# A two-layer hybrid decoder: gates from seven half-size products, seeded accumulators, values and merged sum in DRAM, stages in another order

## The chip, the cores and the metric

The kernel runs on one core of a Trainium2 chip. Its five engines work side by side, each through its own queue: TensorE (PE, with PEld for its weight loads), VectorE (DVE), ScalarE (ACT), GpSimd (POOL) and SyncE (SP, which here only issues transfers). The metric is the time of one execution on the device in microseconds (us). Three executions before took 1969.81, 1969.9 and 1974.25 us, a median of 1969.9.

## The reference

There are 512 tokens with 1024 channels, in float32, and two layers. Cut to what matters:

```python
mod = c_act @ w_ada[l] + b_ada[l]                # 6 x 1024 modulation values
h = rms_norm(x, norm1[l]) * (1.0 + sc1) + sh1
q, k, v, g, u, vs, p, gate_cols = split_columns(h @ w_in[l])
y_ret  = retention(q, k, v, g, positions)        # 4 heads, rotary, decay, rms norm, silu(g)
y_sgu  = spatial_gating(u, vs, ...)              # gelu(u) * (W_s rms_norm(gelu(vs)) + b)
y_pool = multiscale_pool(p, w_pool[l], ...)      # windows 2, 4, 8, 16
branch_proj = einsum('bsnc,ncd->bsnd', stack([y_ret, y_sgu, y_pool]), w_branch[l])
merged = sum(sigmoid(gate_cols) * branch_proj, over the three branches)
x = x + gt1 * (merged @ w_out[l])
h2 = rms_norm(x, norm2[l]) * (1.0 + sc2) + sh2
x = x + gt2 * (square(relu(h2 @ w_ff1[l])) @ w_ff2[l])    # 4096 hidden channels
```

After both layers comes a last rms norm. The gates are 3 x 1024 columns of `w_in`.

## The kernel before

Activations lie channels by tokens: 8 blocks of 128 partitions with 512 tokens. Every large product is made from three, in `mm3` (L405): each float32 operand is split into a high part (ScalarE, `act`, L210) and a low part, the rest (VectorE, `ttn`, L207), and high x high, high x low and low x high are added up in PSUM. So `a_unit`, 128 output channels from 1024 input channels, is 8 x 3 = 24 matmuls of 512 columns.

The weights come in **units** of 128 x 1024 (512 KB), in the order in which they are used. SP loads them (L226) into four buffers. A unit is split as two halves of 512, with eight such half buffers.

`pair` is another way to make two such output blocks at once. It takes them as a 2 x 2 block product (two halves of the tokens, two of the input channels) and makes it from seven half-size products rather than eight: sums S1 to S4 of weight blocks by sums T1 to T4 of activation blocks. Each product is 4 blocks x 3 = 12 matmuls of 256 columns into one of four PSUM banks a, b, c and d; VectorE adds the banks up. The T sums are made once per activation (`Halved.add`), the S sums per pair: S1 and S3 on POOL, S2 and S4 on VectorE (L274). Before, only the first feed-forward product uses pairs, 11 in each layer; the gates are direct units.

The stages of a layer before: v; vs; retention by heads (q, k, g, scores, with `attend` and `attend_norm` of one head during the next); branch 0 (each gate, then its branch product, which VectorE multiplies into `merged`); u with the spatial gating; branch 1; p; the pooling product `wpool`; branch 2; the output product; then the feed-forward part in four quarters of the hidden channels, `ff1` and `ff2` in turn. Between them lie 96 **modulation units**: a unit of `w_ada` is loaded and reduced on VectorE (L245), one after each step that carries `mods=1`.

Order: `run()` goes through the steps, and before each step it has the weights of the next LOOKAHEAD halves loaded and split. A scheduler then places the instructions of each engine, each engine works strictly in that order, and waits only for what an instruction reads or overwrites. At the passages between layers and sub-layers the order is written out by hand (`ordered` steps).

Of the kernel before, what the change touches and what calls it, by code (L numbers as in the profile page):

```python
# [11 lines left out]
F32 = mybir.dt.float32  # L12
# [5 lines left out]
P = 128  # L18
D = 1024
# [96 lines left out]
class Weights:  # L116


    def __init__(self, halves):
        self.halves = halves  # L120

    def part(self, i, o, n):
        return self.halves[o // S][i][:, o % S:o % S + n]
# [8 lines left out]
class Halved:  # L132
# [6 lines left out]
    def add(self, p, f):  # L139

        b = self.b
        upper, lower = f
        r11, r12, r21, r22 = upper[:, :, :HT], upper[:, :, HT:], lower[:, :, :HT], lower[:, :, HT:]
        for names in (("T1", "T2"), ("T3", "T4")):
            raw = b.b4("tsum").rearrange("p a (k s) -> p a k s", k=2)
            x, y = raw[:, 0], raw[:, 1]
            if names[0] == "T1":
                b.ttn(x, r11, r12, ALU.subtract)
                b.ttn(y, r22, x, ALU.add)
                t2 = y  # L150
            else:
                b.ttn(x, r12, r22, ALU.subtract)
                b.ttn(y, r21, t2, ALU.subtract)
            parts = [b.big.tile([P, 2, 2, HT], F32R, tag="b4", name=b.name("tpart")) for _ in range(2)]
            b.act(parts[0], raw, AF.Copy)
            b.ttn(parts[1], raw, parts[0].bitcast(F32), ALU.subtract)
            for i, n in enumerate(names):
                self.sums[n, p] = [t[:, i] for t in parts]
# [9 lines left out]
class Builder:  # L168
    def __init__(self, tc, ctx, ins, out, wstream, order):
# [8 lines left out]
        self.whl = ctx.enter_context(tc.tile_pool(name="whl", bufs=HALF_BUFS))  # L178
# [15 lines left out]
    def tt(self, s="t", dt=F32):  # L194
        return self.tmp.tile([P, S], dt, tag="t", name=self.name(s))

    def bank(self):
        return self.psum.tile([P, S], F32, tag="ps", name=self.name("ps"))

# [29 lines left out]
    def half(self):  # L229
        return tuple(self.whl.tile([P, S], F32R, tag="w" + w, name=self.name("w" + w)) for w in ("hi", "lo"))  # L230

    def split_half(self, src):
        hi, lo = self.half()
        self.act(hi, src, AF.Copy)
        self.ttn(lo, src, hi.bitcast(F32), ALU.subtract)
        return hi, lo

    def load_unit(self, key, early=False):
# [10 lines left out]
        def parts(between=None):  # L249
            src = [raw[:, i * S:(i + 1) * S] for i in range(2)]  # L250
            if between is None:
                return Weights([self.split_half(x) for x in src])
            halves = [self.half() for _ in src]
            for x, (hi, _) in zip(src, halves):
                self.act(hi, x, AF.Copy)

            def low():
                for x, (hi, lo) in zip(src, halves):
                    self.ttn(lo, x, hi.bitcast(F32), ALU.subtract)

            between()
            return Weights(halves), low
# [3 lines left out]
    def load_pair(self, keys):  # L266
# [3 lines left out]
        sums = {}  # L270

        def add(name, x, y, eng):
            sums[name] = self.sums.tile([P, S], F32, tag="sum", name=self.name("sum"))
            eng.tensor_tensor(sums[name], x, y, ALU.add)  # L274
            return sums[name]

        def make(form):
            nc = self.nc
# [987 lines left out]
```

## Time and profile before

The profiled execution took 1971.48 us by the same clock as the runs, with a span of 1969.8 us. The granted TensorE clock is 0.995 of full speed on the mean.

| engine | busy us | share of the span |
|---|---|---|
| PE | 1943.2 | 99% |
| DVE | 1224.8 | 62% |
| ACT | 789.0 | 40% |
| POOL | 85.4 | 4% |

The transfers move 237.95 MB, a mean of 121 GB/s. Busy times of matmuls overlap, so a busy PE is not PE at its peak; what a matmul costs is read from the distance between starts in the timeline. In a row of waits stand engine, tile and line, what it waited for, then total us, number of times and the longest. In a row of groups stand total us and mean ns of one, then the idle time before them and what ended it.

### The profile page before, as it was taken

To read this page: it belongs to the slowest core of one execution; us is meant where nothing else is said; L and a number is where in the kernel's file an instruction comes from. 1 tells how busy PE (TensorE), PEld (TensorE's weight loads), DVE (VectorE), ACT (ScalarE), POOL (GpSimd) and SP (SyncE) were. 2 spreads that over 40 slices of the span, in tenths; PEclk is the share of its full clock that TensorE was granted. 3 is DMA by queue.
4 is the path that set the end of the run, shared out by engine and by line. 5 is a ranking of instruction groups with operands and counts; after the bars stand their busy time and mean duration, and the time that the engine had idled before them with its cause. 6 is when DMAs were issued, how large, how long until landed. Compare 5 with 4: busy or idle time off the path is not lost.

```text
span 1969.8 us, 25044 instructions
## 1 busy us (share of the span) xinstructions
PE 1943.2 (99%) x9632; PEld 1635.6 (83%) x9632; DVE 1224.8 (62%) x2089; ACT 789.0 (40%) x1290; POOL 85.4 (4%) x90
## 2 busy tenths in 40 slices
PE   8999999999999989999999999999999999999998
PEld 5887788788888879898888777888888898899896
DVE  7757755646744697797652675344375458666665
ACT  4434332323433454353534334233243336353442
POOL 2000000000000001111000000000000000102010
PEclk9999999999999999999999999999999999999999
DMA  8322454444323254654423232222232212332331
GB/s 349 127 87 78 148 179 169 151 155 147 97 97 97 72 178 150 201 181 153 137 87 129 86 100 78 101 86 97 97 96 97 96 65 97 107 118 74 120 107 43
DMA packets 67818, 237.95 MB, mean 121 GB/s; under 512 B 7537, under 2 KB 9713, under 8 KB 67698
## 3 DMA queue, kind: packets, MB, share of 16 engines
q1 hardware_dynamic: 67698, 236.35, 35.9%
q8 instruction: 75, 1.23, 0.3%
q14 instruction: 45, 0.37, 0.1%
HBM read 234.23 MB, written 2.10 MB: 120 GB/s over the span
## 4 chain that ended last, share of the span: by engine, by line
PE 93%; DVE 3%; DMA 2%; ACT 1%; issue 1%; SPq 0%; POOL 0%; DVEq 0%; ACTq 0%
PE ps L405 89%; DMA raw<-in_weights 2%; PE ps L792 2%; PE ps L769 1%; PE ps L885 1%; DVE wlo L207 1%; ACT whi L210 0%; PE ps L987 0%; PE ps L805 0%; DVE raw L245 0%; DVE s L207 0%; DVE tsum L207 0%; ACT tpart L210 0%; DVE fo L204 0%; SPq L488 0%
## 5 line engine op out<-in xcount | busy, mean ns | idle before, releaser
L210 ACT ACTIVATE whi<-raw 128x512 fp32r<-128x512 f32 x658 | 406.8, 629 | 798.0 <-PE ps L405 671.8
L207 DVE TENSOR_TENSOR wlo<-raw,whi 128x512 fp32r<-128x512 f32 x658 | 454.9, 700 | 328.1 <-ACT whi L210 324.3
L405 PE MATMUL ps<-h_hi,whi 128*128 128x512 f32 x896 | 356.5, 398 | 0.0
L405 PE MATMUL ps<-h_hi,wlo 128*128 128x512 f32 x896 | 349.9, 391 | 0.0
L405 PE MATMUL ps<-h_lo,whi 128*128 128x512 f32 x896 | 349.6, 390 | 0.0
L405 PE MATMUL ps<-hid_lo,whi 128*128 128x512 f32 (+1 forms) x544 | 204.8, 377 | 0.0
L405 PE MATMUL ps<-hid_hi,wlo 128*128 128x512 f32 (+1 forms) x544 | 204.6, 377 | 0.0
L405 PE MATMUL ps<-hid_hi,whi 128*128 128x512 f32 (+1 forms) x544 | 203.6, 378 | 0.5 <-ACT whi L210 0.5
L405 PEld LDWEIGHTS ps<-h_hi,whi 128*128 128x128 f32 x896 | 168.9, 189 | 36.5 <-issue 2.4
L405 PEld LDWEIGHTS ps<-h_lo,whi 128*128 128x128 f32 x896 | 168.9, 189 | 36.4 <-issue 2.6
L405 PEld LDWEIGHTS ps<-h_hi,wlo 128*128 128x128 f32 x896 | 168.6, 188 | 35.4
L245 DVE CUSTOM_DVE_ANT_0 raw<-raw,cact 128x1024 f32<-128x1024 f32 x96 | 117.3, 1223 | 115.6 <-DMA raw<-in_weights 115.6
L405 PE MATMUL ps<-hh_hi,whi 128*128 128x256 f32 (+1 forms) x456 | 141.0, 315 | 3.1 <-ACT whi L210 3.1
L405 PE MATMUL ps<-hh_lo,whi 128*128 128x256 f32 (+1 forms) x456 | 142.5, 313 | 0.0
L405 PE MATMUL ps<-hh_hi,wlo 128*128 128x256 f32 (+1 forms) x456 | 141.8, 313 | 0.0
L405 PE MATMUL ps<-tpart,whi 128*128 128x256 f32 x704 | 129.3, 285 | 0.0
L405 PEld LDWEIGHTS ps<-hid_hi,whi 128*128 128x128 f32 x544 | 102.4, 188 | 19.1 <-ACT whi L210 0.7
L405 PEld LDWEIGHTS ps<-hid_hi,wlo 128*128 128x128 f32 x544 | 102.4, 188 | 18.6
L405 PEld LDWEIGHTS ps<-hid_lo,whi 128*128 128x128 f32 x544 | 102.4, 188 | 18.4
L405 PEld LDWEIGHTS ps<-tpart,whi 128*128 128x128 f32 x704 | 111.2, 194 | 0.5
L204 DVE SCALAR_TENSOR_TENSOR x<-ps,mod,x 128x512 f32<-128x512 f32 (+1 forms) x88 | 61.3, 700 | 67.4 <-PE ps L405 67.3
L405 PE MATMUL ps<-tpart,wlo 128*128 128x256 f32 x352 | 99.9, 286 | 2.6 <-DVE wlo L207 2.6
(186 smaller groups left out, 3104.8 us busy)
## 6 DMA issues: line engine op xcount, KB each, us to landing
raw<-in_weights SPq DMA_DIRECT2D x436, 512.0 KB, 3.5
x<-in_xT SPq DMA_DIRECT2D x8, 256.0 KB, 4.0
dec<-in_decay SPq DMA_DIRECT2D x4, 512.0 KB, 6.4
out_dram<-fo SPq DMA_DIRECT2D x8, 256.0 KB, 2.1
mix<-in_wsT SPq DMA_DIRECT2D x2, 256.0 KB, 6.9
mix<-in_bs SPq DMA_DIRECT2D x2, 256.0 KB, 6.9
posi<-in_positions SPq DMA_DIRECT2D x1, 256.0 KB, 10.3
vecs<-in_vecs SPq DMA_DIRECT2D x1, 92.0 KB, 1.9
```

The source lines that it names most:

```text
L204: self.nc.vector.scalar_tensor_tensor(out, in0, sc, in1, op0, op1)
L207: self.nc.vector.tensor_tensor(out, a, b, op)
L210: self.nc.scalar.activation(out, in_, f, **k)
L245: self.nc.vector.tensor_tensor_reduce(out=raw, in0=raw, in1=self.cact, scale=0.5, scalar=0.0, op0=ALU.mult, op1=ALU.add, accum_out=acc)
L405: mm(ps, lhsT=l, rhs=r, start=start and i == 0, stop=stop and i == 2, skip_group_check=loose)
L769: nc.tensor.matmul(ps[:, :w], lhsT=k[:, j * P:(j + 1) * P], rhs=q[:, j * P:], start=True, stop=True)
L792: nc.tensor.matmul(ps[:, j * P:], lhsT=st["v"][j][:, col // S, col % S:col % S + P], rhs=sc[j], start=j == 0, stop=j == NCH - 1)
L885: nc.tensor.matmul(mx[:, t * P:(t + 1) * P], lhsT=st["vg"][t][:, c // 4, (c % 4) * P:(c % 4) * P + P], rhs=st["wsr"][t // 2][:, t % 2, g * ...
```

## The change

All three branches' gates are made as pairs (12 in each layer), over T sums of `h` that are made during the vs steps. In the feed-forward part four output blocks of the second quarter become direct units, where two were, so 10 pairs are left there.

Inside `pair` ScalarE seeds accumulators: after the first product bank a is copied to b, product S2 then adds onto b, b is copied to c, and S3, S4 and W2b go onto b, c and b again. Product S1 goes to d and is copied to SBUF, from where VectorE adds it to two outputs. Two PSUM banks form a pool of their own for seeded banks (b and c), and six stay in the old one.

Units are split whole (1024 columns, four buffers), the weight sums are all on VectorE, two of them in place over the loaded unit, and POOL adds nothing. LOOKAHEAD becomes two whole units.

The values v are stored to DRAM after their stage and loaded again by heads; the decay table is loaded for two heads at a time; `merged` is stored to DRAM after branches 1 and 0 and loaded again. The stages become: v, vs, u, branch 1, retention, branch 0, p, `wpool`, branch 2. The square of the direct feed-forward units moves from VectorE to ScalarE, and feed-forward pairs carry no modulation units; branch 1 carries them in both layers and branch 0 in the first only.

```diff
@@ class Weights, constants
-LOOKAHEAD = 4
-HALF_BUFS = 8
-BIG_BUFS = 30
+LOOKAHEAD = 2
+UNIT_BUFS = 4
+BIG_BUFS = 31
-PAIR_AHEAD = 7
-FORMS = ("W1a", "S2", "S1", "S3", "W1b", "S4", "W2b")
+FORMS = {"W1a": (0, 0), "W1b": (0, S), "S1": (1, 0), "S2": (1, S), "S3": (2, 0), "S4": (2, S), "W2b": (3, 0)}
...
@@ class Halved: the sums of the activations
-    def add(self, p, f):
+    def add(self, p, f=None):
+        if f is None:
+            f = []
+            for k2 in (p, p + KB // 4):
+                f.append(b.b4("f32"))
+                hi, lo = (self.act.two(w, k2).bitcast(F32) for w in ("hi", "lo"))
+                b.ttn(f[-1], hi, lo, ALU.add)
...
+        b.ttn(t1, r12, r11, ALU.subtract)
+        b.ttn(t2, r22, t1, ALU.subtract)
+        b.ttn(t3, r22, r12, ALU.subtract)
+        b.ttn(t4, r21, t2, ALU.subtract)
...
@@ pools
-        self.sums = ctx.enter_context(tc.tile_pool(name="sums", bufs=3))
-        self.pairs = ctx.enter_context(tc.tile_pool(name="pairs", bufs=1))
+        self.sums = ctx.enter_context(tc.tile_pool(name="sums", bufs=1))
+        self.dram = ctx.enter_context(tc.tile_pool(name="dram", bufs=1, space=bass.MemoryType.DRAM))
-        self.psum = ctx.enter_context(tc.tile_pool(name="psum", bufs=8, space=bass.MemoryType.PSUM))
+        self.psum = ctx.enter_context(tc.tile_pool(name="psum", bufs=6, space=bass.MemoryType.PSUM))
+        self.seeded = ctx.enter_context(tc.tile_pool(name="seeded", bufs=2, space=bass.MemoryType.PSUM))
...
@@ splitting a unit, and the weight sums of a pair
-    def split_half(self, src):
-        hi, lo = self.half()
-        self.act(hi, src, AF.Copy)
-        self.ttn(lo, src, hi.bitcast(F32), ALU.subtract)
+    def split_unit(self, src):
+        n = src.shape[-1]
+        hi, lo = self.unit()
+        self.act(hi[:, :n], src, AF.Copy)
+        self.ttn(lo[:, :n], src, hi[:, :n].bitcast(F32), ALU.subtract)
+        return Weights(hi, lo)
...
-            if form == "W1a":
-                add("S1", r2[:, a], r2[:, b], nc.gpsimd)
-                add("S3", r1[:, a], r2[:, a], nc.gpsimd)
-                src = r1[:, a]
...
+            if group == 0:
+                return self.split_unit(r1)
+            if group == 1:
+                s = self.sums.tile([P, D], F32, tag="sum", name=self.name("sum"))
+                got.append(s)
+                self.ttn(s[:, a], r2[:, a], r2[:, b], ALU.add)
+                self.ttn(s[:, b], s[:, a], r1[:, a], ALU.subtract)
+                return self.split_unit(s)
+            if group == 2:
+                self.ttn(r1[:, a], r1[:, a], r2[:, a], ALU.subtract)
+                self.ttn(r1[:, b], r1[:, b], got[0][:, b], ALU.subtract)
+                return self.split_unit(r1)
+            return self.split_unit(r2[:, b])
...
@@ pair
-        a, b, c, d = (self.bank()[:, :HT] for _ in range(4))
+        a, b, c, d = (x()[:, :HT] for x in (self.bank, self.ubank, self.ubank, self.bank))
...
         product(a, "W1a", "R11", True)
-        self.act(a1, a, AF.Copy)
-        product(b, "S2", "T2", True)
-        self.ttn(q, b, a1, ALU.subtract)
-        product(c, "S1", "T1", True)
-        self.ttn(r, q, c, ALU.subtract)
-        product(d, "S3", "T3", True)
-        self.ttn(out1[:, h1], r, d, ALU.add)
+        self.act(b, a, AF.Copy)
+        product(d, "S1", "T1", True)
+        self.act(d_sb, d, AF.Copy)
+        product(b, "S2", "T2", False)
+        self.act(c, b, AF.Copy)
         product(a, "W1b", "R21", False)
-        self.act(out0[:, h0], a, f)
+        f(out[:, 0, h0], a)
+        product(b, "S3", "T3", False)
+        self.ttn(out[:, 1, h1], b, d_sb, ALU.add)
         product(c, "S4", "R22", False)
-        self.ttn(out0[:, h1], c, q, ALU.subtract)
-        product(d, "W2b", "T4", False)
-        self.ttn(out1[:, h0], d, q, ALU.add)
+        self.ttn(out[:, 0, h1], c, d_sb, ALU.add)
+        product(b, "W2b", "T4", False)
+        f(out[:, 1, h0], b)
...
@@ mixer: v, T sums of h, retention, gates, branches
-            st["v"] = []
+            st["v"] = self.dram.tile([NCH, P, D], F32, tag="v", name=self.name("v"))
...
-                st["v"].append(vt)
+                nc.sync.dma_start(out=st["v"][t], in_=vt.rearrange("p a s -> p (a s)"))
...
+                if n == 1 and k2 in (0, 2):
+                    hx.add(k2 // 2)
...
+                if what == "q":
+                    if hd % 2 == 0:
+                        self.dec = self.b4("dec")
+                        nc.sync.dma_start(out=self.dec, in_=self.ins["decay"][:, hd:hd + 2, :])
+                    vh = self.b4("vh").rearrange("p a (b e) -> p (a b) e", b=2)
+                    nc.sync.dma_start(out=vh, in_=st["v"][:, :, hd * 256:(hd + 1) * 256].rearrange("t p e -> p t e"))
...
-                ps = self.a_unit(w, h)
-                t = self.tt("gate")
-                self.act(t, ps, AF.Tanh, scale=0.5)
-                st["gate", c] = t
+                g = self.b4("gate")
...
+                self.pair(form, hx, g, tanh, hooks)
+                tanh(g[:, :, HT:], g[:, :, HT:])
...
+                if n != 1 and i == 0 and k2 + 1 < KB // 2:
+                    recall(0 if n == 2 else 1, k2 + 1)
                 ps = self.a_unit(w, y)
...
+                elif i == 1:
+                    nc.sync.dma_start(out=parked[n, k2], in_=merged[k2].rearrange("p a s -> p (a s)"))
...
         def branch(n, y, mods=0):
-            ahead = 3 if n == 0 else 1
+            ahead = 2 if n == 0 else 1
+            for k2 in range(ahead):
+                gates(n, k2, mods)
+            for k2 in range(KB // 2):
+                for c in (2 * k2, 2 * k2 + 1):
+                    self.step([("A", "w_branch", l, n, 0, c * P)], branch_step(n, y, c), mods=mods)
+                if k2 + ahead < KB // 2:
+                    gates(n, k2 + ahead, mods)
-        branch(0, yret, mods=1)
...
-        branch(1, ysgu, mods=1 if l == 0 else 0)
+        branch(1, ysgu, mods=1)
+        retention()
+        branch(0, yret, mods=1 if l == 0 else 0)
...
+        for k2 in range(KB // 2):
+            for j in ((0,), (1, 2, 3), (), ())[k2]:
+                gates(2, j)
+            if k2 == 0:
+                self.step([("P", "w_pool", l, 1, 0, 0)], wpool_step(4))
+            for c in (2 * k2, 2 * k2 + 1):
+                self.step([("A", "w_branch", l, 2, 0, c * P)], branch_step(2, ypool, c))
...
@@ channel mixer
-            self.ttn(s, r, r, ALU.mult)
+            self.act(s, r, AF.Square)
...
-                if (q, k2) == (1, 0):
-                    for c in range(2):
-                        self.step([wff1(q, c)], ff1_step(q, c), mods=1)
+                if q == 1 and k2 < 2:
+                    for c in (2 * k2, 2 * k2 + 1):
+                        self.step([wff1(q, c)], ff1_step(q, c))
                 else:
-                    self.step([("pair", wff1(q, 2 * k2), wff1(q, 2 * k2 + 1))], ff1_pair(q, k2), mods=1)
+                    self.step([("pair", wff1(q, 2 * k2), wff1(q, 2 * k2 + 1))], ff1_pair(q, k2))
```

Three places of the order.

VectorE, end of the u steps and begin of the second branch in layer 0 (`ysg` and `ysgu0_lo3` are the last block of that branch's input, `wlo` low parts of weights, `raw ... cact` with `acc` and `mod` a modulation unit). Before:

```order
L245 ISA raw_594_3010,acc0_96<-raw_594_3010,cact_100 128x1024
L245 ISA acc0_96 128x1
L207 TENSOR_TENSOR wlo_576_2921<-raw_574_2918,whi_575_2920 128x512
L313 TENSOR_TENSOR mod0_98<-acc0_96,vecs_83 128x1
L207 TENSOR_TENSOR wlo_578_2925<-raw_574_2918,whi_577_2924 128x512
L204 SCALAR_TENSOR_TENSOR ysg_565_2872<-ps_564_2867,vecs_83,mix_128_662 128x512
L207 TENSOR_TENSOR ysg_565_2872<-ysg_565_2872,gu_563_2865 128x512
L207 TENSOR_TENSOR ysgu0_lo3_2824<-ysg_565_2872,ysgu0_hi3_2822 128x512
```

After:

```order
L256 ISA raw_236_1416,acc0_98<-raw_236_1416,cact_102 128x1024
L256 ISA acc0_98 128x1
L217 TENSOR_TENSOR wlo_227_1352<-raw_204_1224,whi_226_1351 128x512
L304 TENSOR_SCALAR mod0_100<-acc0_98,vecs_85 128x1
L214 SCALAR_TENSOR_TENSOR ysg_217_1308<-ps_216_1303,vecs_85,mix_107_623 128x512
L305 TENSOR_TENSOR mod0_100<-mod0_100,vecs_85 128x1
L217 TENSOR_TENSOR ysg_217_1308<-ysg_217_1308,gu_215_1301 128x512
L217 TENSOR_TENSOR ysgu0_lo3_1267<-ysg_217_1308,ysgu0_hi3_1265 128x512
L217 TENSOR_TENSOR sum_243_1483<-raw_238_1436 128x512
L217 TENSOR_TENSOR sum_243_1483<-sum_243_1483,raw_237_1434 128x512
```

Before, a modulation unit and two half splits stand ahead of the last block; now a modulation unit and one half split do, and behind it come the weight sums (`sum`) of a gate pair.

SP, second branch in layer 0 after the change (`raw` are weight units, `parked` the place of `merged` in DRAM):

```order
L236 DMA raw_290_1800<-in_weights 128x1024
L236 DMA raw_291_1818<-in_weights 128x1024
L236 DMA raw_294_1824<-in_weights 128x1024
L886 DMA parked_7_113<-merged_270_1660 128x1024
L236 DMA raw_295_1841<-in_weights 128x1024
L236 DMA raw_296_1843<-in_weights 128x1024
L236 DMA raw_315_1966<-in_weights 128x1024
```

The store of the second part of `merged` now stands between unit loads. It waits for VectorE's last product into `merged_270_1660`, and the load behind it (`raw_295_1841`) for the buffer of `raw_267_1640`, which VectorE's next instruction sets free:

```order
L217 TENSOR_TENSOR wlo_274_1691<-sum_272_1687,whi_273_1690 128x1024
L305 TENSOR_TENSOR mod0_100<-mod0_100,vecs_85 128x1
L217 TENSOR_TENSOR wlo_283_1743<-raw_266_1638,whi_282_1742 128x1024
L214 SCALAR_TENSOR_TENSOR merged_270_1660<-gate_247_1517,ps_275_1694 128x512
L217 TENSOR_TENSOR wlo_285_1760<-raw_267_1640,whi_284_1759 128x512
L256 ISA raw_294_1824,acc0_98<-raw_294_1824,cact_102 128x1024
```

The fourth row is that product and the fifth the instruction that frees the buffer.

ScalarE in a run of feed-forward pairs of layer 0 (`whi` high parts of weights, `pair` the outputs, `hid0_2_hi2` their high part, `a1` the copy of bank a; after the change `us` are the seeded banks and `d` the copy of bank d). Before:

```order
L210 ACTIVATE whi_1379_7271<-sum_1371_7216 128x512
L210 ACTIVATE pair_1330_7033<-pair_1330_7033 128x1024
L210 ACTIVATE whi_1381_7288<-raw_1368_7210 128x512
L210 ACTIVATE hid0_2_hi2_7178<-pair_1330_7033 128x1024
L210 ACTIVATE whi_1384_7307<-sum_1383_7305 128x512
L210 ACTIVATE whi_1393_7337<-raw_1369_7212 128x512
L210 ACTIVATE whi_1397_7360<-raw_1396_7358 128x512
L210 ACTIVATE pair_1358_7182<-ps_1359_7183 128x256
L210 ACTIVATE a1_1391_7335<-ps_1387_7331 128x256
L210 ACTIVATE whi_1399_7364<-raw_1396_7358 128x512
```

After:

```order
L220 ACTIVATE us_994_6248<-ps_993_6247 128x256
L220 ACTIVATE d_997_6251<-ps_996_6250 128x256
L220 ACTIVATE whi_1004_6318<-raw_1002_6314 128x1024
L220 ACTIVATE us_995_6249<-us_994_6248 128x256
L220 ACTIVATE whi_1007_6338<-sum_1006_6335 128x1024
L220 ACTIVATE pair_992_6246<-ps_993_6247 128x256
L220 ACTIVATE whi_1009_6357<-raw_1002_6314 128x1024
L220 ACTIVATE pair_992_6246<-pair_992_6246 128x2x256
L220 ACTIVATE us_1013_6382<-ps_1012_6381 128x256
L220 ACTIVATE d_1016_6385<-ps_1015_6384 128x256
```

Before, one copy of bank a stands among half splits, and VectorE takes the other sums from the banks. Now three copies are made per pair, the one of bank b to c (`us_995_6249<-us_994_6248`) behind the whole split `whi_1004_6318` of the next pair.

More of the change, by code (lines that the diff above doesn't have):

```diff
@@ L249, in parts @@
         def parts(between=None):
-            src = [raw[:, i * S:(i + 1) * S] for i in range(2)]
             if between is None:
[L252 to L259, printed above, removed]
+                return self.split_unit(raw)
+            hi, lo = self.unit()
+            self.act(hi, raw, AF.Copy)
             between()
-            return Weights(halves), low
+            return Weights(hi, lo), lambda: self.ttn(lo, raw, hi.bitcast(F32), ALU.subtract)
         return mod if key[0] == "mod" else parts
@@ L330, in run @@
             for k in keys:
[L331 removed]
+                pieces += [(k, g) for g in range(4)] if k[0] == "pair" else [(k, None)]
             pieces += [(mod_queue.pop(0), None) for _ in range(min(mods, len(mod_queue)))]
```

232 lines of the change are left out of this document (106 added, 126 removed).

## The prediction

> **What bounds the kernel now.** I read the page's totals first, then the chain of waits, then TensorE's waits, then single stages.
>
> ```profile
> span 1969.8 us, 25044 instructions
> PE 1943.2 (99%) x9632; PEld 1635.6 (83%) x9632; DVE 1224.8 (62%) x2089; ACT 789.0 (40%) x1290; POOL 85.4 (4%) x90
> ...
> PE 93%; DVE 3%; DMA 2%; ACT 1%; issue 1%; SPq 0%; POOL 0%; DVEq 0%; ACTq 0%
> ```
>
> TensorE is busy all the time and is 93% of the chain. So the time falls only by fewer or cheaper matmuls, or by the waits that TensorE still has:
>
> ```profile
> PE ps L405 <- ACT whi L210: 3.6, 8, 1.0
> PE ps L405 <- ACT ysgu_hi L210: 3.5, 1, 3.5
> PE ps L405 <- DVE wlo L207: 2.6, 1, 2.6
> PE ps L474 <- DMA cin<-in_c: 2.3, 1, 2.3
> PE ps L805 <- DVE osq L204: 1.7, 1, 1.7
> ```
>
> The other five rows of that view add 4.2, so all waits are 17.9 us of the span. The rest is matmuls back to back, and what one costs is its spacing in the timeline, not its "busy" mean (matmuls overlap):
>
> ```profile
> 602.77 0.39 PE L405 MATMUL ps<-mrg_lo,whi 128*128 128x512 f32 x1
> ...
> 608.89 0.39 PE L405 MATMUL ps<-mrg_lo,whi 128*128 128x512 f32 x1
> 839.15 0.28 PE L405 MATMUL ps<-hh_hi,whi 128*128 128x256 f32 x1
> ...
> 844.90 0.28 PE L405 MATMUL ps<-hh_hi,whi 128*128 128x256 f32 x1
> ```
>
> The first two rows are 27 steps apart: 6.12/27 = 0.2267 us for 512 columns. The second two are 48 steps apart (four products of twelve): 5.75/48 = 0.120 us for 256 columns.
>
> How near the other engines are to TensorE is read by stage. The columns are length, then busy time of PE, PEld, DVE, ACT and POOL, then the granted clock, the DMA share and GB/s:
>
> ```profile
> 134.00:251.00 117.00, 115.28 (x485) 88.88 (x484) 82.51 (x146) 46.16 (x68) 0.00 (x0) 1.00 0.33 109
> 373.00:461.00 88.00, 84.53 (x360) 68.92 (x359) 47.54 (x92) 25.10 (x44) 0.11 (x1) 0.96 0.51 168
> 690.00:722.00 32.00, 26.87 (x145) 22.73 (x144) 31.56 (x54) 20.15 (x38) 3.45 (x2) 0.95 0.33 109
> 839.00:877.00 38.00, 38.00 (x316) 37.92 (x315) 35.56 (x62) 23.41 (x40) 6.75 (x4) 1.00 0.49 161
> ```
>
> The rows are the v and vs steps, the second branch, the passage into the first FF pair, and a run of FF pairs, all of layer 0. VectorE is full only in the third (31.56 of 32), and there TensorE falls behind. At 35.56 of 38 TensorE is still full.
>
> **Matmuls.** A pair is 7 products of 12 matmuls of 256 columns, 84 x 0.120 = 10.08 us, in place of two direct units, 48 x 0.2267 = 10.88. It gains 0.80. The instruction order has 6860 matmuls of 512 columns before and 5804 after, 2464 of 256 before and 4312 after, the rest alike: 1056 go, 1848 come, which is 22 pairs (24 gate pairs in, 2 FF pairs out). 1056 x 0.2267 - 1848 x 0.120 = 239.4 - 221.8, so **-17.6**. All of it lies on the bounding engine.
>
> The Trainium skill ("TensorE: Matmul & The Clock Gate", "Back-to-back issue gap") gives columns/2.4 + 2.5 ns as the gap of isolated matmuls. By it 215.8 and 109.2 ns, 227.9 - 201.8 = 26.1 us saved and a result near 1949; the rows are 5% and 10% longer here, so the measurement decides.
>
> **Stalls that go.** Two of the waits stand where the change rearranges work. The second branch:
>
> ```profile
> 376.39 1.23 DVE L245 CUSTOM_DVE_ANT_0 raw<-raw,cact 128x1024 f32<-128x1024 f32 x1 [2.03 <-DMA raw<-in_weights]
> 377.54 0.08 DVE L245 DVE_READ_ACCUMULATOR2_ANT acc<- 128x1 f32 x1
> ...
> 378.14 0.15 DVE L313 TENSOR_TENSOR mod<-acc,vecs 128x1 f32<-128x1 f32 x1
> ...
> 381.07 0.79 PE L405 MATMUL ps<-ysgu_hi,whi 128*128 128x512 f32 x1 [3.47 <-ACT ysgu_hi L210]
> ```
>
> VectorE sat 2.03 us on a modulation unit's load, then made two weight splits, and only then the last block of `ysgu`; one direct gate (24 x 0.2267 = 5.4 us) did not cover that. The stage's clock of 0.96 is another 0.04 x 88 = 3.5. After the change a gate pair of 10.1 us stands there, 4.6 us more cover than a 3.5 us wait needs: **-7.0**. The other is the first FF pair:
>
> ```profile
> 710.23 0.38 PE L405 MATMUL ps<-tpart,wlo 128*128 128x256 f32 x1 [2.55 <-DVE wlo L207]
> ...
> 712.01 0.63 PE L405 MATMUL ps<-tpart,whi 128*128 128x256 f32 x2
> 712.43 0.41 PE L405 MATMUL ps<-tpart,wlo 128*128 128x256 f32 x1
> ```
>
> Two matmuls take 0.42 there, 0.21 each, nearly twice 0.120: the clock is halved behind a 2.55 us wait (0.95 over the 32 us is 1.6 more). The change puts four direct units ahead of that pair and takes eight squares and the modulation units off VectorE: **-4.2**.
>
> The Trainium skill ("TensorE: Matmul & The Clock Gate", "Part 1: The HAM clock gate") puts the fall to half clock behind an idle window of about 3.4 us; here 2.55 us sufficed, so I price every wait of 2.5 us and more with a half clock behind it. By the page alone waits under 3.4 us would cost only themselves, and the third rival below would come to about 1961 (12.0 of waits in place of 8.0).
>
> **What VectorE and ScalarE get.** Durations by group:
>
> ```profile
> L207 DVE TENSOR_TENSOR hid_lo<-pair,hid_hi 128x1024 fp32r<-128x1024 f32 x22 | 26.9, 1223 | 4.5 <-ACT hid_hi L210 4.2
> L207 DVE TENSOR_TENSOR wlo<-raw,whi 128x512 fp32r<-128x512 f32 x658 | 454.9, 700 | 328.1 <-ACT whi L210 324.3 <-PE ps L405 0.8
> L207 DVE TENSOR_TENSOR merged<-merged,gate 128x512 f32<-128x512 f32 x32 | 22.0, 686 | 0.0
> L207 DVE TENSOR_TENSOR pair<-ps,qr 128x256 f32<-128x256 f32 x44 | 18.3, 418 | 20.1 <-PE ps L405 20.1
> L274 DVE TENSOR_TENSOR sum<-sum,raw 128x512 f32<-128x512 f32 x44 | 37.7, 856 | 9.9 <-POOL sum L274 9.4
> L245 DVE CUSTOM_DVE_ANT_0 raw<-raw,cact 128x1024 f32<-128x1024 f32 x96 | 117.3, 1223 | 115.6 <-DMA raw<-in_weights 115.6
> L210 ACT ACTIVATE hid_hi<-pair 128x1024 fp32r<-128x1024 f32 x22 | 23.1, 1050 | 0.2
> L210 ACT ACTIVATE whi<-raw 128x512 fp32r<-128x512 f32 x658 | 406.8, 629 | 798.0 <-PE ps L405 671.8 <-issue 73.2 <-DMA raw<-in_weights 41.7
> L210 ACT ACTIVATE a<-ps 128x256 f32<-128x256 f32 x22 | 8.1, 368 | 0.0
> L210 ACT ACTIVATE r<-ps 128x512 f32<-128x512 f32 x20 | 11.3, 597 | 4.8 <-PE ps L405 3.4 <-DVE hid_lo L207 1.2
> L210 ACT ACTIVATE sq<-x 128x512 f32<-128x512 f32 (+1 forms) x48 | 25.9, 557 | 38.6 <-DVE x L204 37.7 <-DVE ntot L207 0.9
> raw<-in_weights SPq DMA_DIRECT2D x436, 512.0 KB, 3.5
> dec<-in_decay SPq DMA_DIRECT2D x4, 512.0 KB, 6.4
> ```
>
> VectorE in one FF pair after: three whole-unit low parts 3 x 1.223, one half 0.700, four weight sums 4 x 0.686, two outputs 2 x 0.418, the hidden low part 1.223: 9.17 of TensorE's 10.08, 91%, under the 94% of the run of pairs that was full. (The old weight sums took 0.856 beside POOL's; at that price it would be 9.85, still under 10.08.) ScalarE has 3 x 1.050 + 0.629 for splits, five copies and outputs of 256 columns at 0.368, one relu at about 0.597, square and high part at 1.050 each: 8.3 of 10.08. A gate pair with its two products and three modulation units: 7.95 + 3 x (1.223 + 0.08 + 0.15) + 2 x (1.223 + 0.686) = 16.1 of 10.08 + 2 x 5.44 = 20.96. One load's wait as long as the row of a unit's load (3.5) fits into the 4.9 us left. So I charge VectorE nothing in the steady stages. The T sums of `h` (8 additions at 0.686, 4 low parts and 4 additions of 1024 columns at 1.223, 15 us a layer) go into the v and vs steps, where 117 - 82.5 = 34 us are free: nothing; without that cover, up to 30 us.
>
> The 48 more transfers (v stored and loaded by heads, `merged` parked) are 24 MB on queues that are busy a third of the time. Each parking store waits on SP for a VectorE product, with weight loads queued behind it; but in the order the load next behind waits for the very next VectorE instruction, so the store holds up nothing. A load of v or decay (6.4 us at worst) is issued with its head's q step, and `scores`, the first to need it, comes three units, 16 us, later. Nothing again; if a load did come late, some 3.5 us each.
>
> **New waits,** none of them in the trace, so bounded by rows:
> - At the end of FF quarter 0, ScalarE now does relu, square, high part (0.597 + 0.557 + 0.629) for eight blocks among splits of 1.05, and the next units wait for banks and high parts: 0 to 6 a layer; I take 3, for two layers 6.0, less the 3.6 of `whi` waits that stand mostly there: **+2.4**.
> - Within a run of FF pairs (3, 4 and 3 a layer) the seed `c` is copied from `b` after product S2, and S3 overwrites `b` 12 x 0.120 = 1.44 us later. In the order one split stands ahead of the copy: 1.05 + 0.37 + 0.1 = 1.52, so 0.08 late, filled by two matmuls of the next pair; a second split would make it 1.13. I take 0.35, nearer the low end, on the 14 pairs that have a predecessor: **+4.9**. (The other seed, of `b` from `a`, has only itself, 0.37, to do in the 1.44 of product S1: nothing.)
> - Branch 0 now follows retention with all gate pairs around the last head's `attend`; the nearest row is the 1.7 of `osq`: 0 to 4.5 (with half clock) a layer, taken 1.5: **+3.0**.
> - From `p` through `wpool` into three gate pairs in a row (VectorE makes pools, splits and sums there); the nearest row is the 2.6 of the first FF pair: 0 to 4.5, taken 2.5 a layer: **+5.0**.
> - The first unit is split whole: 1.050 - 0.629 + 1.223 - 0.700: **+0.9**.
>
> Sum on the profiled execution, whose own time is 1971.5: 1971.5 - 17.6 - 7.0 - 4.2 + 2.4 + 4.9 + 3.0 + 5.0 + 0.9 = 1958.9. That execution lies 1.6 over the median of 1969.9, so **1957**.
>
> **Rivals.**
> 1. No new wait at all: 1971.5 - 28.8 - 1.6 = 1941, or 1943 with half a microsecond lost here and there. For it: every new wait sits beside slack of several microseconds in the steady stages. Against: a queue in program order keeps a late item in front. 0.18.
> 2. Slower: the accumulator hand-off. If two splits stand in front of the copy of `b` in every pair, 2 x 1.05 + 0.37 - 1.44 = 1.03 us a pair, 44 pairs: 1957 - 4.9 + 45.3 = 1997. It decides from (1969.9 - 1952.4)/44 = 0.40 us a pair. For it: the copy exists nowhere in the old pair, where four banks let each product be read at leisure. Against: only one split stands there in the order. 0.14, reaching down to 1976.
> 3. No change: the gain is given back at transitions. Waits of 3 us with half a clock of 1.6 behind at the four places of the third and fourth point, 18.4 in place of 8.0: 1957 + 10.4 = 1968. For it: both stalls of before were of this kind. Against: pairs give twice the cover of a direct gate. 0.20.
>
> That the change would not remove the matmuls is excluded by the counts.
>
> **How the numbers follow.** The forecast, 1946 to 1966, has 0.48. A measurement of this kernel tells 0.3%, 5.9 us, from no change: bounds 1964.0 and 1975.8. Faster: rival 1 and nine tenths of the forecast, 0.18 + 0.43, and a tenth of rival 3, 0.02: 0.63. Same: 0.05 of the forecast, 0.16 of rival 3: 0.21. Slower: rival 2, 0.14, and a tenth of rival 3, 0.02: 0.16. The range, 1942 to 1976, takes in rivals 1 and 3, leaves out the slower one and a little below. The ends of all bounds together are 1941 and, with 0.5 for each of 44 pairs, 6 and 18 for the transitions, about 1988.
>
> **What would show it.** TensorE's matmul spacing stays 0.227 and 0.120; the waits on `ysgu_hi` and on the first FF pair's `wlo` are gone; waits on the seeded banks appear in FF runs with some 0.3 us each; the granted clock is 1.00 in the second branch. VectorE stays under 95% in FF runs. Wrong it would be if TensorE waited half a microsecond or more in each pair, if waits on DMA or on parked tiles appeared, or if spacing within a pair grew.

## The result and the profile after

The changed kernel took 1986.8 us (median of four runs, 1984.92 to 1987.02) against 1971.3 (1969.81 to 1974.25): a ratio of 1.0075, with a 95% interval of 1.0057 to 1.0092. The forecast was 1957 with a range of 1942 to 1976. It is slower, and not by the mechanism of any of the three rivals.

The page of the changed kernel, totals and chain:

```profile
span 1984.9 us, 25937 instructions
...
PE 1930.0 (97%) x10424; PEld 1660.5 (84%) x10424; DVE 1293.1 (65%) x1895; ACT 817.4 (41%) x1156; POOL 19.7 (1%) x46
...
PE 89%; DVE 5%; DMA 3%; ACT 2%; issue 1%; SPq 0%; POOL 0%; DVEq 0%; ACTq 0%
```

TensorE is 89% of the chain, where it was 93%, and VectorE and the transfers stand there with 5% and 3%. TensorE's waits say for what:

```profile
PE ps L912 <- DVE wsr L1182: 28.3, 2, 16.0
PE ps L406 <- ACT r L220: 7.0, 2, 3.5
PE ps L477 <- DMA cin<-in_c: 2.4, 1, 2.4
PE us L406 <- DVE pair L217: 1.3, 2, 1.1
...
PE us L406 <- ACT us L220: 0.9, 2, 0.5
...
PE ps L406 <- DVE wlo L217: 0.7, 3, 0.3
PE ps L406 <- ACT whi L220: 0.7, 2, 0.6
```

All waits add up to 45.2 us (three rows of 1.3, 1.1 and 0.9 and three of 0.2 are not shown), against 17.9 before. The span grew by 15.1. With the 17.6 that the matmul counts save, 32.7 have to be found: 27.3 are more waits. The remaining 5.4 were not placed: the granted clock is lower, 0.990 on the mean against 0.995, but that mean also counts time in which TensorE only waited.

The first row is new. `wsr` are the weights of the spatial gating, scaled by the statistics of vs, one wait in each layer. The stretch of the first one in the windows (columns as in the prediction):

```profile
96.00:132.00 36.00, 19.96 (x88) 16.29 (x87) 32.21 (x54) 12.40 (x15) 0.00 (x0) 0.80 0.54 167
```

TensorE is busy for 20 of 36 us, VectorE for 32. TensorE's timeline there:

```profile
114.45 0.39 PE L406 MATMUL ps<-h_hi,wlo 128*128 128x512 f32 x1
130.87 0.79 PE L912 MATMUL ps<-wsr,vg 128*128 128x128 f32 x2 [16.04 <-DVE wsr L1182]
131.32 0.77 PE L406 MATMUL ps<-h_hi,whi 128*128 128x512 f32 x1
131.89 0.63 PE L406 MATMUL ps<-h_lo,whi 128*128 128x512 f32 x1
```

and VectorE's, with ScalarE's last gelu of vs ahead of it:

```profile
111.96 0.58 ACT L220 ACTIVATE vg<-ps 128x512 f32<-128x512 f32 x1
```

```profile
112.62 1.23 DVE L256 CUSTOM_DVE_ANT_0 raw<-raw,cact 128x1024 f32<-128x1024 f32 x1 [1.66 <-DMA raw<-in_weights]
...
117.39 1.23 DVE L256 CUSTOM_DVE_ANT_0 raw<-raw,cact 128x1024 f32<-128x1024 f32 x1 [0.54 <-DMA raw<-in_weights]
...
118.54 1.22 DVE L217 TENSOR_TENSOR tpart<-tsum,tpart 128x1024 fp32r<-128x1024 f32 x1
119.67 1.22 DVE L1173 CUSTOM_DVE_ANT_0 junk<-vg 128x1024 f32<-128x1024 f32 x1
...
125.64 1.22 DVE L1173 CUSTOM_DVE_ANT_0 junk<-vg 128x1024 f32<-128x1024 f32 x1
...
128.48 1.23 DVE L256 CUSTOM_DVE_ANT_0 raw<-raw,cact 128x1024 f32<-128x1024 f32 x1 [1.41 <-DMA raw<-in_weights]
...
130.33 1.67 DVE L1182 TENSOR_SCALAR wsr<-mix,vss 128x512 f32<-128x512 f32 x4
```

The last block of vs is there at 112.5. Then VectorE has modulation units, T sums and weight splits in its queue, makes the four sums of squares (`junk`) from 119.67 to 126.8, and `wsr` from 130.33. TensorE came to the first mixing matmul at 114.8, since u now follows vs directly, and everything behind it waited.

Before, the same matmul came 200 us later, and the row was in the trace of before:

```profile
116.19 1.68 DVE L1153 TENSOR_SCALAR wsr<-mix,vss 128x512 f32<-128x512 f32 x4
```

```profile
321.91 1.05 PE L885 MATMUL ps<-wsr,vg 128*128 128x128 f32 x8
```

`wsr` was ready at 117.9 and first used at 321.9, with retention and branch 0 between. That cover is what the new order of the stages took away.

The move alone does not give the size of the wait. In the trace of before vs ends here, and the next unit begins:

```profile
110.42 0.39 PE L405 MATMUL ps<-whi,h_lo 128*128 128x512 f32 x1
110.65 0.39 PE L405 MATMUL ps<-h_hi,whi 128*128 128x512 f32 x1
```

From there to the first `wsr` at 116.19 are 5.5 us, and one unit is 5.4. With VectorE's queue as it was, u directly behind vs would have waited about half a microsecond (an estimate: the first of the four `wsr` ends 0.5 after its start). After the change the first matmul of u starts at 109.23 and `wsr` at 130.33, 21.1 us later. So both are new: that the result is needed at once, and some 16 us more that VectorE does or waits for ahead of it: modulation units, which the u steps carry and the retention steps did not, their loads, T sums and weight splits of whole units.

What the prediction said would go did go: no wait on `ysgu_hi` and none over 0.3 us on `wlo` is left.

### The profile page after: what moved, and what is told of

The parts are those of the page before. It is cut to its first block, busy times and chain, and to the rows that moved or that the text cites. A ratio compares the mean times of both kernels' runs of the same rounds, so it can differ in the third digit from the quotient of the medians.

```text
span 1984.9 us, 25937 instructions
## 1 busy us (share of the span) xinstructions
PE 1930.0 (97%) x10424; PEld 1660.5 (84%) x10424; DVE 1293.1 (65%) x1895; ACT 817.4 (41%) x1156; POOL 19.7 (1%) x46
## 4 chain that ended last, share of the span: by engine, by line
PE 89%; DVE 5%; DMA 3%; ACT 2%; issue 1%; SPq 0%; POOL 0%; DVEq 0%; ACTq 0%
PE ps L406 71%; PE us L406 14%; DMA raw<-in_weights 2%; PE ps L800 2%; DVE wlo L217 1%; DVE raw L256 1%; ACT whi L220 1%; PE ps L778 1%; PE ps L912 1%; PE ps L1016 0%; DVE f L217 0%; DVE junk L1173 0%; PE ps L813 0%; DMA v<-v 0%; ACT pair L220 0%
## 5 line engine op out<-in xcount | busy, mean ns | idle before, releaser
L220 ACT ACTIVATE whi<-raw 128x1024 fp32r<-128x1024 f32 (+1 forms) x384 | 385.6, 1008 | 741.5 <-PE ps L406 494.0
L217 DVE TENSOR_TENSOR wlo<-raw,whi 128x1024 fp32r<-128x1024 f32 (+1 forms) x384 | 443.5, 1160 | 190.5 <-ACT whi L220 183.7
L406 PE MATMUL ps<-h_hi,whi 128*128 128x512 f32 (+1 forms) x704 | 260.3, 370 | 0.0
L406 PE MATMUL ps<-h_hi,wlo 128*128 128x512 f32 (+1 forms) x704 | 255.2, 362 | 0.0
L406 PE MATMUL ps<-h_lo,whi 128*128 128x512 f32 (+1 forms) x704 | 254.8, 362 | 0.0
L406 PE MATMUL us<-tpart,whi 128*128 128x256 f32 x1056 | 196.2, 284 | 2.3 <-DVE pair L217 1.3
L406 PEld LDWEIGHTS us<-tpart,whi 128*128 128x128 f32 x1056 | 167.6, 191 | 8.2 <-DVE pair L217 1.7
L406 PEld LDWEIGHTS ps<-h_hi,whi 128*128 128x128 f32 x704 | 133.8, 190 | 21.5 <-issue 1.4
L406 PEld LDWEIGHTS ps<-h_lo,whi 128*128 128x128 f32 x704 | 133.7, 190 | 21.5 <-issue 1.4
L406 PE MATMUL us<-tpart,wlo 128*128 128x256 f32 x528 | 149.4, 283 | 0.0
L406 PEld LDWEIGHTS ps<-hid_hi,whi 128*128 128x128 f32 x544 | 102.4, 188 | 19.2 <-ACT whi L220 0.7
```

The source lines that it names most:

```text
L217: self.nc.vector.tensor_tensor(out, a, b, op)
L220: self.nc.scalar.activation(out, in_, f, **k)
L406: mm(ps, lhsT=l, rhs=r, start=start and i == 0, stop=stop and i == 2, skip_group_check=loose)
```

## Experiments

Times are medians; the kernel before ran beside each set at 1972.2 to 1972.5, so the sets can be compared directly. Ratios are to it, with the 95% interval. The theory was (A) that the stage move makes the wait; rivals were (B) the T sums, (C) the modulation units in front of the statistics, and (D) loss inside the pairs.

**Late mixing matmuls.**

```diff
+U_TAIL = ((), (), (), (0, 1), (2, 3), (4, 5), (6,), (7,))
...
         def u_step(c):
             def f(w):
                 ps = self.a_unit(w, h)
                 gu = self.tt("gu")
                 self.act(gu, ps, AF.Gelu_apprx_tanh)
+                gus[c] = gu
+                for cc in U_TAIL[c]:
+                    u_tail(cc)
+            return f
+
+        def u_tail(c):
+                gu = gus.pop(c)
                 g = c // 2
...
```

Block 0 comes three units later, blocks 1 and 2 two, blocks 3 and 4 one.

> Edit: in the u stage the mixing matmuls of blocks 0 to 3 (those that read wsr, the scaled mixing weights) are issued two or three units later, all else as in the changed kernel. Theory A (the stage move: TensorE reaches the first mixing matmul one unit after vs, before VectorE has made the vs statistics): the waits on wsr, 28.3 us in the profile of the changed kernel, and some 3 us of half clock behind them go: 1986.8 - 31 = about 1956, and no wait on wsr over 1 us. Theory D (the time is lost inside the pairs, by accumulator hand-offs): under 10 us gained, 1977 or more.

Measured 1960.35, 0.994 (0.9925 to 0.9955): 26.5 us less than the changed kernel, and 0.6% faster than before. That is 4 us more than theory A's 1956. The same stretch:

```profile
96.00:132.00 36.00, 36.00 (x161) 29.81 (x160) 33.08 (x55) 16.90 (x20) 0.00 (x0) 1.00 0.58 185
```

TensorE is full at full clock, while VectorE does as much as in the changed kernel. No wait on `wsr` is left; 2.8 us of waits on `whi` in the two u stages are new. D falls as the cause of the slowdown; what the pairs lose is measured below. A holds in that the matmul's place decides whether TensorE waits. What makes `wsr` late is the question of the next runs.

**T sums behind the statistics.**

```diff
-                if n == 1 and k2 in (0, 2):
-                    hx.add(k2 // 2)
...
                 self.act(gu, ps, AF.Gelu_apprx_tanh)
+                if c in (2, 5):
+                    hx.add(c // 3)
```

> Edit: the T sums of h are made during u steps 2 and 5 in place of the vs steps, so VectorE has them behind the vs statistics and not before. Theory A (the stage move): after the last gelu of vs the statistics, two or three weight splits and two modulation units are still some 12 us of VectorE against 5 us of cover, so 5 to 8 us of wait stay in each layer: about 1970. Theory B (the T sums in front are the whole cause): both waits on wsr go, about 1957.

Measured 1985.39, 1.0067 (1.0052 to 1.0082): 1.4 us less than the changed kernel, which is not clear of the noise (the runs of the two overlap). Both theories expected more. The wait is 25.3 still:

```profile
PE ps L912 <- DVE wsr L1182: 25.3, 2, 13.0
```

```profile
104.88 1.23 DVE L256 CUSTOM_DVE_ANT_0 raw<-raw,cact 128x1024 f32<-128x1024 f32 x1 [4.24 <-DMA raw<-in_weights]
...
111.39 1.23 DVE L256 CUSTOM_DVE_ANT_0 raw<-raw,cact 128x1024 f32<-128x1024 f32 x1 [4.02 <-DMA raw<-in_weights]
```

VectorE now stands idle where the T sums were, in front of modulation units whose loads have not landed, and the statistics are behind them in its queue. B as the whole cause falls.

**First u steps without modulation units.**

```diff
-            self.step([win(OFF_U + c * P)], u_step(c), mods=1)
+            self.step([win(OFF_U + c * P)], u_step(c), mods=0 if c < 3 else 1)
```

(and `mods=1` on the first three steps of retention)

> Edit: the first three u steps carry no modulation unit; the first three steps of retention do. Theory C (modulation units and their loads in front of the statistics are the cause): layer 0 gains 3 x 1.45 + 3.6 of load waits = 8 us, layer 1 about 5: about 1973. Theories A and B: they are only one part of the queue in front of wsr, the gain is at most that and something else on VectorE stays late; the waits on wsr keep more than half of their 28.3 us.

Measured 1975.81, 1.0019 (1.0009 to 1.0028): 11.0 us gained, the wait on `wsr` halved to 14.3. So these three modulation units are about half of it. Others are still in front: in layer 0 this run has modulation units at 108.52, 113.55 and 120.53, ahead of `wsr` at 122.78.

**Both of the last two edits.**

> Edit: the first three u steps without modulation units and the T sums made in u steps 2 and 5, both, in the changed kernel. If T sums and modulation units add up in front of the vs statistics, 3 us or more a layer less than with the first alone (1975.8): under 1970. If the T sums only fill time in which VectorE would wait (as the run with late T sums says): within 2 us of 1975.8.

Measured 1966.13, 0.9969 (0.9959 to 0.9979): 9.7 us less than without modulation units alone, and the wait is down to 7.2. My reading after the run with late T sums, that the T sums only fill idle time, was wrong. They do so only while the loads of the modulation units are in front; once three of these are gone, the T sums are part of what VectorE is late with. Removing one of two causes in the same queue gave 1.4 or 11.0, removing both 20.7. The 7.2 that stay are not the statistics alone. In layer 0 two modulation units still stand ahead of and among them, `wsr` begins at 119.69, and TensorE came at 116.7:

```profile
107.94 1.23 DVE L256 CUSTOM_DVE_ANT_0 raw<-raw,cact 128x1024 f32<-128x1024 f32 x1 [4.45 <-DMA raw<-in_weights]
115.03 1.23 DVE L256 CUSTOM_DVE_ANT_0 raw<-raw,cact 128x1024 f32<-128x1024 f32 x1 [0.70 <-DMA raw<-in_weights]
```

**Direct gates, the mixing matmuls at their place.**

```diff
-                self.pair(form, hx, g, tanh, hooks)
-                tanh(g[:, :, HT:], g[:, :, HT:])
+                for i, w in enumerate(ws):
...
+                    self.act(g[:, i, :], self.a_unit(w, h), AF.Tanh, scale=0.5)
```

(and no T sums of `h`)

> Edit: the changed kernel with direct gates and no T sums of h, the mixing matmuls at their place. Theory A (the stage move alone makes the wait on wsr, whatever the gates are): 25 us or so above the same kernel with late mixing matmuls (1970.9), about 1996. Rival (the pairs' extra VectorE work makes most of it): under 1985.

Measured 2001.04, 1.0148 (1.0133 to 1.0163).

```profile
PE ps L905 <- DVE wsr L1175: 26.0, 2, 14.1
```

With no gate pair and no T sum of `h` in the kernel the wait is there in nearly full size. This is 30.1 us above the next kernel, which differs in the place of the mixing matmuls alone. So the wait does not come from the pairs: with u directly behind vs it is there whatever the gates are. VectorE stands idle in front of a modulation unit here too, and the statistics begin at 114.81, behind it; before, they began at 107.40:

```profile
112.40 1.23 DVE L256 CUSTOM_DVE_ANT_0 raw<-raw,cact 128x1024 f32<-128x1024 f32 x1 [4.14 <-DMA raw<-in_weights]
```

No run has the new order of stages with VectorE's queue of before, nor the old order with all else changed, so how much each part of the queue adds is shown only as far as the runs above go.

**Direct gates, late mixing matmuls.**

> Edit: as the run with late mixing matmuls, and the gates are made as direct units again (no T sums of h). If the pairs give what the matmul counts say, this is 24 x 0.80 = 19 us slower than the run with late mixing matmuls, about 1975. Theory D (hand-offs eat the gain): within 5 us of it.

Measured 1970.93, 1.0 (0.9991 to 1.001). The gate pairs with their T sums are worth 10.6 us, not 19.2 and not nothing.

**Bank order in the feed-forward part.** The second row of the waits, 3.5 us on `r` in each layer: the first direct unit behind quarter 0 takes the bank of the third relu, since the first two blocks sit in seeded banks.

```diff
-                        st["fps"][c] = self.ubank() if c < 2 else self.bank()
+                        st["fps"][c] = self.ubank() if c in (5, 6) else self.bank()
```

> Edit: as the run with late mixing matmuls (1960.4); in quarter 0 of the feed-forward part blocks 5 and 6 take the two seeded banks, in place of blocks 0 and 1, so the first direct unit behind it gets the bank of the first relu and not that of the third. Theory F (the two waits of 3.5 us on r are a matter of which bank the next unit gets): both go, with the half clock behind them, about 5 us a layer: 1951. Theory E (ScalarE is too slow there with eight squares more): the wait turns up at the next units, under 4 us gained.

Measured 1949.70, 0.9887 (0.9872 to 0.9902): 10.7 us less than with late mixing matmuls alone, and no wait on `r` at all. Theory F (bank order) holds.

**Square back on VectorE.**

```diff
-            self.act(s, r, AF.Square)
+            self.ttn(s, r, r, ALU.mult)
```

> Edit: as the run with late mixing matmuls (1960.4); the square of the direct feed-forward units is back on VectorE. Theory E (ScalarE's squares are the cause of the waits on r): the 7.0 us go, about 1952. Theory F (bank order, and a split ahead of the second relu): of what stands before the third relu only two squares go, 1.2 us a layer; 2 to 3 us gained, about 1958.

Measured 1953.72, 0.991 (0.9893 to 0.9926): 6.6 us less, more than F said and less than E. The wait went from 7.0 to 3.9, about as F counted. The rest is the clock behind it. In layer 0, behind the wait of 3.50 us with late mixing matmuls alone, and behind that of 1.94 us in this run:

```profile
682.00:690.00 8.00, 8.00 (x29) 6.39 (x29) 5.52 (x13) 8.00 (x16) 0.00 (x0) 0.79 0.60 188
```

```profile
680.00:690.00 10.00, 10.00 (x46) 8.27 (x45) 10.00 (x19) 7.71 (x14) 0.00 (x0) 1.00 0.58 170
```

The first loses 0.21 x 8 = 1.7 us to the clock, the second nothing; for two layers that is 3.4 (an estimate from layer 0), and 3.1 + 3.4 = 6.5 is nearly the whole gain.

**Unseeded pairs.**

```diff
-        self.act(b, a, AF.Copy)
+        self.act(a1, a, AF.Copy)
         product(d, "S1", "T1", True)
-        self.act(d_sb, d, AF.Copy)
-        product(b, "S2", "T2", False)
-        self.act(c, b, AF.Copy)
+        product(b, "S2", "T2", True)
+        self.ttn(q, b, a1, ALU.add)
         product(a, "W1b", "R21", False)
         f(out[:, 0, h0], a)
-        product(b, "S3", "T3", False)
-        self.ttn(out[:, 1, h1], b, d_sb, ALU.add)
-        product(c, "S4", "R22", False)
-        self.ttn(out[:, 0, h1], c, d_sb, ALU.add)
-        product(b, "W2b", "T4", False)
-        f(out[:, 1, h0], b)
+        self.ttn(qd, d, q, ALU.add)
+        product(c, "S3", "T3", True)
+        self.ttn(r, c, q, ALU.add)
+        self.ttn(out[:, 1, h1], d, r, ALU.add)
+        product(b, "S4", "R22", True)
+        self.ttn(out[:, 0, h1], b, qd, ALU.add)
+        product(c, "W2b", "T4", True)
+        self.ttn(out[:, 1, h0], c, r, ALU.add)
+        f(out[:, 1, h0], out[:, 1, h0])
```

> Edit: as the run with late mixing matmuls (1960.4); a pair no longer seeds accumulators, VectorE adds the banks up (four more operations of 0.42 us on it, three copies fewer on ScalarE, in each of 44 pairs). By the prediction's count VectorE gets 9.17 + 1.67 = 10.84 of TensorE's 10.08 us in a feed-forward pair: 20 x 0.76 = up to 15 us slower, 1965 to 1975. Rival (seeding is worth nothing, its hand-offs cost what it saves): within 3 us of 1960.

Measured 1953.74, 0.991 (0.9895 to 0.9924): 6.6 us *faster*, against both expectations. The same stretch of feed-forward pairs, with seeding and then without:

```profile
740.00:800.00 60.00, 58.09 (x372) 52.62 (x371) 39.69 (x60) 28.36 (x41) 0.00 (x0) 1.00 0.46 150
```

```profile
740.00:800.00 60.00, 60.00 (x385) 54.80 (x384) 45.64 (x73) 26.58 (x35) 0.00 (x0) 1.00 0.50 161
```

VectorE has 6 us more to do, and TensorE is full. In the seeded kernel (with late mixing matmuls) TensorE and VectorE there:

```profile
770.92 0.51 PE L407 MATMUL us<-tpart,whi 128*128 128x256 f32 x2 [1.20 <-DVE pair L218]
774.29 0.50 PE L407 MATMUL us<-tpart,whi 128*128 128x256 f32 x2 [0.47 <-ACT us L221]
```

```profile
768.10 1.22 DVE L218 TENSOR_TENSOR hid_lo<-pair,hid_hi 128x1024 fp32r<-128x1024 f32 x1
769.24 0.69 DVE L218 TENSOR_TENSOR raw<-raw,raw 128x512 f32<-128x512 f32 x1
769.84 0.69 DVE L218 TENSOR_TENSOR raw<-raw,sum 128x512 f32<-128x512 f32 x1
770.44 0.42 DVE L218 TENSOR_TENSOR pair<-us,d 128x256 f32<-128x256 f32 x1
```

The bank that seeding keeps in use has to be read by VectorE between two of its products, with one product of 1.44 us as cover, and that read stands behind a low part of 1.22 and two weight sums. Unseeded, bank b is read with two products as cover. Bank c still has one (`r`, between S3 and W2b): waits on `qr`, 3.7 us in three gate pairs, are new, but none shows in feed-forward pairs. Why this read is in time there was not worked out.

The gain lies in layer 0. At the wait on `r` ahead of its feed-forward pairs the two runs stand at 681.76 and 681.60; at the first mixing matmul of layer 1, with seeding and then without, they are 5.3 us apart:

```profile
1097.13 1.05 PE L922 MATMUL ps<-wsr,vg 128*128 128x128 f32 x8
```

```profile
1091.78 0.49 PE L926 MATMUL ps<-wsr,vg 128*128 128x128 f32 x2 [0.33 <-DVE wsr L1195]
```

Between them lie ten feed-forward pairs and no gate pair. VectorE was not over full, as the expectation had it. The run of four pairs, with seeding and then without:

```profile
825.00:863.00 38.00, 36.87 (x301) 36.14 (x300) 25.68 (x35) 24.56 (x40) 0.00 (x0) 1.00 0.35 105
```

```profile
822.00:858.50 36.50, 36.50 (x304) 36.42 (x303) 30.76 (x48) 21.35 (x30) 0.00 (x0) 1.00 0.29 93
```

That is 68% and 84% of the time, where the counts of 9.17 and 10.84 in 10.08 say 91% and 108%.

**Late mixing matmuls, bank order, unseeded pairs.**

> Edit: late mixing matmuls, the other bank order and unseeded pairs together. If the two gains (10.7 and 6.6 us against the run with late mixing matmuls alone) have different places and add: 1943. If they overlap: 1946 or more.

Measured 1943.48, 0.9854 (0.9838 to 0.9871). The gains add (1943 expected), and this is 1.5% faster than the kernel before. With the square on VectorE too:

> Edit: late mixing matmuls, the other bank order, unseeded pairs, and the direct square on VectorE. Theory F (bank order was all of the waits on r): within 1.5 us of the same without the square moved. Theory E (ScalarE is still short there): 3 us or more faster.

Measured 1942.86, 0.9853 (0.9838 to 0.9868): no difference, as theory F says.

**The same without gate pairs.**

> Edit: the run before this, with direct gates and no T sums of h. By the matmul counts 24 x 0.80 = 19 us slower than it. If what the gate pairs gave back earlier (19.2 counted, 10.6 measured) was in the seeding, now near 19; if it lies in the T sums and the whole-unit weight sums, again near 11.

"The run before this" is the one of 1943.48, with the square on ScalarE. Measured 1953.85, 0.9906 (0.9891 to 0.9921): the pairs are worth 10.4 us here, as with seeding. So what they give back of the 19.2 is not in the seeding. One stretch of layer 0, vs to the second branch, of the version with pairs and then of the one without:

```profile
100.00:250.00 150.00, 147.00 (x832) 128.64 (x831) 116.92 (x195) 57.36 (x77) 0.00 (x0) 1.00 0.54 176
```

```profile
100.00:250.00 150.00, 150.00 (x695) 125.41 (x694) 84.44 (x138) 44.67 (x57) 0.00 (x0) 1.00 0.53 179
```

With pairs VectorE has 32 us more to do there, and TensorE loses 3 us; in layer 1 the first gate pair of that branch waits 2.38 us:

```profile
1125.08 0.39 PE L407 MATMUL us<-h_hi,whi 128*128 128x256 f32 x1 [2.38 <-DVE qr L218]
```

The granted clock behind that wait is 0.89 over 15 us, another 1.6 us; without gate pairs it is 1.00 there:

```profile
1120.00:1135.00 15.00, 12.62 (x71) 11.25 (x70) 10.91 (x19) 4.71 (x7) 0.00 (x0) 0.89 0.52 175
```

That places some 7 of the 8.8 us in these stretches, most of it where the second branch begins. The rest was not placed.

## Why the prediction was wrong, point by point

The step that failed is the list under "New waits". It goes through four passages and the start, and leaves out the one where the change puts u directly behind vs; the wait there is in no term and in no rival. It was let through by the charge of "nothing" for VectorE, and there a row was misread. The window 134 to 251, called the v and vs steps, begins 24 us after the last vs matmul (110.42): it is retention and the begin of branch 0. The v and vs steps of layer 0, with the end of the start, lie in this one, with 23 us free in place of 34:

```profile
10.00:111.00 101.00, 97.88 (x402) 76.67 (x403) 77.61 (x131) 43.74 (x75) 17.38 (x25) 0.98 0.58 219
```

That is an average over stages all the same. What mattered was the one unit, 5.4 us, between the last matmul of vs and the first use of `wsr`. The trace of before shows that `wsr` took 5.5 us from there, so there was room for nothing more on VectorE; the change added some 16 us in layer 0. The two waits are 28.3 us in the trace; the run that removes them gains 26.5 (with 2.8 of new waits on `whi`), and the two runs with direct gates differ by 30.1. The T sums' price "without that cover, up to 30 us" is near these by chance: without the T sums alone the time fell by 1.4, and without T sums and gate pairs the wait was still 26.0.

With that wait away the kernel takes 1960.4, against 1957 forecast, but not by the terms being right one by one:

- **Matmuls, -17.6.** Their number and spacing came as counted. Measured alone, the 24 gate pairs gain 10.4 to 10.6 of the 19.2 counted for them; some 7 of the other 8.8 are given back behind VectorE, most of it at the begin of the second branch. "I charge VectorE nothing in the steady stages" was too good by that.
- **Stalls that go, -7.0 and -4.2.** Both went: no row for `ysgu_hi`, 0.7 left on `wlo`. (The 3.5 us of clock count some 0.5 twice: over 377.6 to 381.0, while TensorE waited, the clock was 0.86 already.)
- **End of quarter 0, +2.4 net.** Right in place and mis-sized: 3 a layer was near the 3.5 measured, but I left out the half clock behind it, against my own rule for waits of 2.5 us and more. The run with the other bank order shows 10.7 for both layers where I had 6.0. The cause was not ScalarE's load alone: the next unit took the bank of the third relu.
- **Seeded accumulators, +4.9.** Near in size (6.6), wrong in part about the place: I watched ScalarE's copy (0.9 us of waits in all), and the longer wait is for VectorE's read of the same bank. And the cost is not spread over 14 pairs: 5.3 of it lie in the ten feed-forward pairs of layer 0. Why layer 1 loses so little there stays open. The VectorE count of 9.17 a pair was too high for these short runs (68% busy, not 91%).
- **Branch 0, +3.0, and wpool to gates, +5.0.** Neither shows: no wait on `osq` is left, and the waits over the whole kernel on `wlo` and `whi` are 1.4.
- **First unit, +0.9.** No row shows it.
- **Transfers at nothing.** Right as far as the rows show: no TensorE wait names a parked tile, v or decay, with stores of `merged` landing in 3.3 us and loads in 5.2. (The 6.4 taken as the worst for v or decay was a median; here the loads of v take 5.7 in the median.)

Rival 3 had the right kind of loss (gains given back at transitions) at four places that do not include the real one, and at 3 us where one wait was 16.0. The time lies where rival 2 reached, between 1976 and 1997, but not by its mechanism: seeding cost 6.6 us in all, 0.15 a pair on the mean and not 1.03. That "slower" got the 0.14 of its chance by this rival was luck.

## What to carry to other kernels

When stages are reordered, write down for each result that crosses a stage when it is made and when it is first used, from the trace of before; a result that is ready 200 us early may have lived on that cover, and its producer's whole queue counts, not only its own instructions. Free time of an engine summed over a stage does not cover a need at its end; check, too, that the window is that stage. An accumulator that is seeded or reused inside a group adds a read that must be on time between two products, so ask what stands ahead of that read in its engine's queue, and look at which bank the next work takes.

## What the runs showed that was not expected

Two causes in one queue did not add: T sums away gave 1.4 us (within the noise), three modulation units away 11.0, both 20.7. And the order of eight blocks over the PSUM banks alone was worth 10.7 us, 0.5%: two waits of 3.5 us and the half clock behind them.
